# Hybrid encoder layer on one core: which buffers the first weight loads of the two down stages use, which queue writes the last sums of h, and in what order loads are asked for

## Chip, cores and metric

The kernel runs on one core of a Trainium2 chip. The metric is the device time of one execution in microseconds (us), the median of several runs. The core's engines are TensorE (PE in the profile, its weight loads PEld), VectorE (DVE), ScalarE (ACT), GpSimd (POOL) and SyncE (SP). A DMA is issued by an engine and stands in that engine's queue: "SPq" is what SP issues, "ACTq" what ScalarE issues. "L284" is line 284 of the kernel.

## The reference, cut to what matters

One encoder layer in float32 on 768 tokens (a prompt of 256 and a sample of 512), model width 1024. It has two feed-forward parts (FFN) around a mixer and a cross attention, each followed by a layer norm:

```python
def swiglu(x, w_gu, w_down):
    gate, up = jnp.split(x @ w_gu, 2, axis=-1)      # w_gu: 1024 x 5632
    return (jax.nn.silu(gate) * up) @ w_down        # w_down: 2816 x 1024

x = layer_norm(DN_ALPHA * x + 0.5 * swiglu(x, ffn1_w_gu[l], ffn1_w_down[l]), ...)
x = layer_norm(DN_ALPHA * x + parallel_mixer(x, ...), ...)
x = layer_norm(DN_ALPHA * x + memory_cross_attention(x, mem, ...), ...)
x = layer_norm(DN_ALPHA * x + 0.5 * swiglu(x, ffn2_w_gu[l], ffn2_w_down[l]), ...)
```

The change touches the second product of `swiglu`, `h @ w_down`, in both FFNs. There are thus two down stages, one near 340 us and one near 1630 us.

## The kernel before

**Precision.** Every float32 operand is split in a high and a low part (`split`: ScalarE copies the high part at L87, VectorE or GpSimd subtracts it at L88). A product is three matmuls: high by high, high by low, low by high. So a weight block `raw` becomes `wh` and `wl`, an activation becomes `hq` (both parts in one tile) or `ao`.

**The gate part** of an FFN makes the hidden units in 22 blocks j of 128 (all 768 tokens), with a scheme of seven products in place of eight on half matrices. TensorE writes into banks px, py, pz (L472), ScalarE snaps copies of them (`snap`, L477), VectorE adds them (`sum`, L484), ScalarE takes the SiLU (`sil`, L544), VectorE multiplies (`h`, L545). `gated` then splits h into `hq`, writes it to memory (`hspill`; not for the last four blocks, which stay on chip in `keep`), and for each pair of blocks makes four sums of its quarters (`hs`, L575 to L578), which go to memory as well (`sspill`). The sums of the very last block are not written where they are made: their stores are put in the list `late` and asked for inside `down_seven`, on SP's queue.

**The down part** is `down_seven` for 16 of the 22 blocks, in four groups d = 0 to 3, and `down_last` for the other six. In `down_seven` the products come in this order, each 18 matmuls of 128 x 512 at L284 into banks dn:

- 8 direct products: P1(0), P2(0), P1(1), P2(1), P1(2), P2(2), P2(3), P1(3). Group 0 takes its activations from `keep`, the others load them (768 KB, tile `ao`, a ring of four);
- sums V: four products on `y`, activations loaded as sums (384 KB, tile `sr`, three buffers) and split into `ao`; their weights are T, four kept blocks, plus a newly loaded one (L331);
- sums U, eight products (weights T again, L337, and a loaded block), sums Y, four (weights a sum of two loaded blocks);
- the last four direct products.

`add` (L294, L296) adds the banks into `acc`, the result, whose old values `load_acc` loads late, on ScalarE's queue (L1215).

Weight blocks of 512 KB are loaded by `loaded`. Of five in a row, two go into the buffers `raw7` of this function's own pool, three into the buffers with the tag "raw", which all weights of the kernel share; the pools' order decides what a load has to wait for, since the memory of `raw7` and of the T and ao tiles was used by the gate part before:

```python
            def loaded(q, d):
                turn[0] += 1
                if turn[0] % 5 < 2:
                    r = raw[turn[0] % 5]
                else:
                    r = wp.tile([128, 1024], F32, tag="raw", bufs=3, name=nid("raw"))
```

So the 1st, 5th, 6th, 10th, ... load takes a buffer of `raw7`. `ahead` loads the activations of `down_last` (`hr`, in the first stage four blocks, in the second six) before the last four direct products.

**What sets the order.** The kernel is written as a program, and a scheduler with buffers puts each engine's instructions in an order of its own; within one engine (and one queue) they then run in that order. `tc.issue_after(m)` makes the scheduler place instructions no earlier than m. `late_load` keeps its DMAs in program order. What stands behind a waiting DMA on a queue waits too.

Of the kernel before, what the change touches and what calls it, by code (L numbers as in the profile page):

```python
# [7 lines left out]
F32 = mybir.dt.float32  # L8
# [3 lines left out]
ALU = mybir.AluOpType  # L12
# [7 lines left out]
NFB = D_FF // 128  # L20
# [38 lines left out]
def _encoder(ctx, tc, nc, io, out, dbg):  # L59
# [158 lines left out]
            j = 2 * kp + kk  # L218
            tok_mm(ps, w, kk, hh[s.name, t, j], hl[s.name, t, j], first and kk == 0, stop and kk == 1, cols)

    def down_seven(n, wdn, pairs, keep, dr, sd, order6, load_acc, late, ahead):

        with tc.tile_pool(name=f"seven{n}", bufs=1, reuse_waits="tile") as pool:
            V = nc.vector
            nd = len(pairs)
            raw = [pool.tile([128, 1024], F32, name=nid("raw7")) for _ in range(2)]
            turn = [0]  # L230
            T = {d: pool.tile([128, 1024], F32, name=nid("T")) for d in range(nd)}
            bank = [psum(nid("dn")) for _ in range(8)]
            x, z, y = bank[0:3], bank[3:6], bank[6:8] + bank[3:4]

            def quadrant(dst, q, d):
                row, half = q
                kp = pairs[d][0]
                nc.sync.dma_start(dst.rearrange("p (a c) -> p a c", a=2),
                                  wdn[kp:kp + 2, half, :, row * 512:row * 512 + 512].rearrange("a p c -> p a c"))

            def loaded(q, d):
                turn[0] += 1
                if turn[0] % 5 < 2:
                    r = raw[turn[0] % 5]
                else:
                    r = wp.tile([128, 1024], F32, tag="raw", bufs=3, name=nid("raw"))
                quadrant(r[:], q, d)
                return r[:]
# [10 lines left out]
            def direct(t, par, d):  # L259

                if d == 0:
                    return [keep[2 * kp + par][:, t] for kp in pairs[d]]
                a = ring()
                kp = pairs[d][0]
                nc.sync.dma_start(a[:].bitcast(F32), dr[:, t, par, kp:kp + 2])
                return [a[:, k] for k in range(2)]

            def summed(s, d):
                r = pool.tile([128, 2, HT], F32, tag="sr", bufs=3, name=nid("sr"))
                kp = pairs[d][0]  # L270
                nc.sync.dma_start(r[:], sd[:, s, kp:kp + 2])
                a = ring()
                split(a[:, :, 0, :], a[:, :, 1, :], r[:])
                return [a[:, k] for k in range(2)]
# [25 lines left out]
            B11, B21, B12, B22 = (0, 0), (1, 0), (0, 1), (1, 1)  # L300
# [19 lines left out]
                P2(d)  # L320
            P2(own[-1])
            P1(own[-1])
            for spill in late:
                spill()
            for d in early:
                quadrant(T[d][:], B11, d)
            load_acc(1, 1)
            add(0, 0, z)
            add(0, 0, x)
            for d in sums_:  # L330
                V.tensor_tensor(T[d][:], T[d][:], loaded(B12, d), op=ALU.add)  # L331
                product(y, summed(0, d), weight(T[d][:]), d == sums_[0], d == sums_[-1])
            load_acc(0, 1)
            add(1, 1, y)
            for d in sums_:
# [5 lines left out]
                product(y, summed(2, d), weight(b22), False, d == sums_[-1])  # L341
            load_acc(1, 0)
            add(0, 1, y)
            for d in sums_:
                b12, b22 = loaded(B12, d), loaded(B22, d)
                V.tensor_tensor(b12, b12, b22, op=ALU.add)
                product(x, summed(3, d), weight(b12), False, d == sums_[-1])
            add(1, 1, x)
            ahead()
            for d in own:  # L350
                V.tensor_tensor(T[d][:], T[d][:], loaded(B21, d), op=ALU.add)
                product(x, direct(1, 1, d), weight(T[d][:]), False, d == own[-1])
# [158 lines left out]
    def ffn_fast(n, i, front, order6, src, groups, last):  # L511
# [35 lines left out]
            marks["dve"] = ins.ins  # L547
            gated(j, h32)

        h_of, late = {}, []  # L550

        def hq_tile(hs):
            if n == 1:
# [5 lines left out]
        def gated(j, h32):  # L559

            kp, par = j // 2, j % 2
            whole = par or kp in last
            hs = 2 if whole else 1
            h3 = h32[:].rearrange("p (t c) -> p t c", t=2)
            q = hq_tile(hs)
            split(q[:, :, 0, :], q[:, :, 1, :], h3[:, :hs, :])
            keep[j] = q
            h_of[j] = h3
            if j < NFB - 4:
                nc.sync.dma_start(dr[:, :hs, par, kp], q.bitcast(F32))  # L570
            if par and kp not in last:
                V = nc.vector
                (a11, a21), (a12, a22) = [[h_of[x][:, t, :] for t in range(2)] for x in (j - 1, j)]
                s_ = [glob["hs"].tile([128, HT], F32, tag="hs", bufs=3, name=nid("hs")) for _ in range(4)]
                V.tensor_tensor(s_[3][:], a11, a21, op=ALU.subtract)  # L575
                V.tensor_tensor(s_[0][:], a22, a21, op=ALU.subtract)
                V.scalar_tensor_tensor(s_[1][:], s_[0][:], -1.0, a11, ALU.mult, ALU.subtract)
                V.scalar_tensor_tensor(s_[2][:], s_[1][:], -1.0, a12, ALU.mult, ALU.subtract)  # L578

                def spill():  # L580
                    for x in (3, 0, 1, 2):
                        nc.sync.dma_start(sd[:, x, kp, :], s_[x][:])

                if j == NFB - 1:
                    late.append(spill)
                else:
                    spill()

        def plain_weights(j):
            rg, ru = [wp.tile([128, 1024], F32, tag="raw", bufs=3, name=nid("raw")) for _ in range(2)]  # L590
# [67 lines left out]
        else:  # L658
            lp = hlp.enter_context(tc.tile_pool(name="hlast", bufs=1, reuse_waits="tile"))
            ahead = lambda: load_h(js, lp, "hr", 6)  # L660
        down_seven(n, wdn, groups, keep, dr, sd, order6, load_acc, late, ahead)

        with tc.tile_pool(name=f"down{n}", bufs=1, reuse_waits="tile") as f2:
            if n == 1:
# [783 lines left out]
```

## Time and profile before

| | |
|---|---|
| median of 3 runs | 1814.77 us (1810.16 to 1815.77) |
| profiled execution | 1809.75 us, of which the span in the profile 1808.0 us |
| mean granted TensorE clock | 0.991 |
| TensorE busy | 1762.3 us, 97% of the span |
| weight loads of TensorE busy | 1618.6 us, 90% |
| VectorE busy | 1216.4 us, 67% |
| ScalarE busy | 763.8 us, 42% |
| DMA, mean | 148 GB/s |

The rows that the next parts show come from a timeline (start, us, engine, line, operation, output and inputs, and in brackets the engine's idle time ahead of the row and what ended it), from the list of waits (total us, number, longest), from the list of DMA issues (KB of one, median us from issue to landing) and from windows (length, then for each engine busy us and count, then granted clock, share of the 16 DMA engines, GB/s).

### The profile page before, as it was taken

Reading aid. Unit: us, or ns where it says so; the run is one execution under the profiler, and the core shown is the slowest. Engines: PE = TensorE matmul, PEld = TensorE weight load, DVE = VectorE, ACT = ScalarE, POOL = GpSimd, SP = SyncE. Lnnn points to the kernel's source line nnn. Section 1 sums busy time; section 2 is a strip of 40 time slices with the busy share of each in tenths; the row PEclk is TensorE's granted clock in tenths of the full one; section 3 lists DMA queues with packets and bytes.
Section 4 is the critical chain, followed back from the end, with each engine's and each line's share of the span. In section 5 each row is a group of like instructions: output and inputs, shape, how many; then the busy total and the mean of one; then the engine's idle time right before and its main releaser. Section 6 shows DMA issues by size and latency. Waiting matters only on the chain. (4 is left out here: it accounts for less than half of the span.)

```text
span 1808.0 us, 25217 instructions
## 1 busy us (share of the span) xinstructions
PE 1762.3 (97%) x9758; PEld 1618.6 (90%) x9758; DVE 1216.4 (67%) x2035; ACT 763.8 (42%) x1297; POOL 321.7 (18%) x186
## 2 busy tenths in 40 slices
PE   9999999899999999999999999999999999988998
PEld 9999999788889999888888888889899999986886
DVE  8777777377579553577664934585697777754856
ACT  6444454243135544645322244235344444432421
POOL 2000000000224002422244253244430000000012
PEclk9999999899999999999999999999999999998999
DMA  5434333597432333311463252255424343329951
GB/s 193 143 128 157 135 134 104 186 344 253 185 105 94 123 132 125 104 47 41 132 213 117 83 192 66 80 186 176 140 96 154 128 144 131 127 85 346 334 179 70
DMA packets 100535, 267.26 MB, mean 148 GB/s; under 512 B 10016, under 2 KB 23584, under 8 KB 100416
## 3 DMA queue, kind: packets, MB, share of 16 engines
q1 hardware_dynamic: 93504, 250.46, 39.9%
q10 hardware_dynamic: 6912, 15.21, 2.3%
q8 instruction: 76, 1.25, 0.3%
q14 instruction: 43, 0.35, 0.1%
HBM read 212.15 MB, written 53.48 MB: 147 GB/s over the span
## 5 line engine op out<-in xcount | busy, mean ns | idle before, releaser
L88 POOL TENSOR_TENSOR wl<-raw,wh 128x1024 fp32r<-128x1024 f32 (+1 forms) x94 | 231.6, 2468 | 1319.7 <-ACT wh L87 1271.4
L87 ACT ACTIVATE wh<-raw 128x512 fp32r<-128x512 f32 (+2 forms) x309 | 255.5, 830 | 330.0 <-PE to L108 81.6
L88 DVE TENSOR_TENSOR wl<-raw,wh 128x512 fp32r<-128x512 f32 (+2 forms) x215 | 182.8, 853 | 99.6 <-ACT wh L87 99.3
L284 PE MATMUL dn<-wh,ao 128*128 128x512 f32 x600 | 185.4, 389 | 0.0
L106 PE MATMUL pt<-xh,wh 128*128 128x512 f32 (+2 forms) x512 | 173.1, 338 | 0.0
L107 PE MATMUL pt<-xl,wh 128*128 128x512 f32 (+2 forms) x512 | 172.3, 337 | 0.0
L108 PE MATMUL pt<-xh,wl 128*128 128x512 f32 (+2 forms) x512 | 172.0, 336 | 0.0
L284 PEld LDWEIGHTS dn<-wh,ao 128*128 128x128 f32 x600 | 112.6, 188 | 23.5
L87 ACT ACTIVATE wh<-tt 128x512 fp32r<-128x512 f32 x156 | 95.3, 625 | 78.8 <-PE px L472 36.7
L284 PE MATMUL dn<-wl,ao 128*128 128x512 f32 x300 | 116.7, 389 | 0.0
L88 DVE TENSOR_TENSOR wl<-tt,wh 128x512 fp32r<-128x512 f32 x156 | 105.5, 689 | 2.2 <-ACT wh L87 0.5
L106 PEld LDWEIGHTS pt<-xh,wh 128*128 128x128 f32 x512 | 97.0, 189 | 9.7 <-issue 0.5
L108 PEld LDWEIGHTS pt<-xh,wl 128*128 128x128 f32 x512 | 97.0, 189 | 9.0
L107 PEld LDWEIGHTS pt<-xl,wh 128*128 128x128 f32 x512 | 97.1, 190 | 8.8 <-issue 0.2
L472 PE MATMUL px<-xh,wl 128*128 128x384 f32 x232 | 77.5, 334 | 0.0
L472 PE MATMUL px<-xh,wh 128*128 128x384 f32 x232 | 77.5, 334 | 0.0
L472 PE MATMUL px<-xl,wh 128*128 128x384 f32 x232 | 77.5, 334 | 0.0
L545 DVE SCALAR_TENSOR_TENSOR h<-sil,sum 128x384 f32<-128x384 f32 x78 | 43.5, 557 | 47.1 <-ACT sil L544 47.1
L544 ACT ACTIVATE sil<-sum 128x384 f32<-128x384 f32 x39 | 20.5, 526 | 125.9 <-DVE sum L484 125.9
L284 PEld LDWEIGHTS dn<-wl,ao 128*128 128x128 f32 x300 | 56.3, 188 | 11.8
L106 PE MATMUL dn<-wh,hr 128*128 128x512 f32 (+1 forms) x150 | 57.7, 385 | 0.0
L107 PE MATMUL dn<-wl,hr 128*128 128x512 f32 (+1 forms) x150 | 57.5, 383 | 0.0
(374 smaller groups left out, 4866.4 us busy)
## 6 DMA issues: line engine op xcount, KB each, us to landing
raw<-in_ffn_gu_dram SPq DMA_DIRECT2D x84, 512.0 KB, 3.5
raw<-in_ffn_dn_dram SPq DMA_DIRECT2D x64, 512.0 KB, 5.2
hspill<-hq SPq DMA_DIRECT2D x24, 768.0 KB, 3.7
raw<-in_w_mix_dram SPq DMA_DIRECT2D x32, 512.0 KB, 3.5
ao<-hspill SPq DMA_DIRECT2D x18, 768.0 KB, 5.7
sspill<-hs SPq DMA_DIRECT2D x64, 192.0 KB, 2.1
sr<-sspill SPq DMA_DIRECT2D x32, 384.0 KB, 5.7
hr<-hspill SPq DMA_DIRECT2D x24, 384.0 KB, 5.6
```

The costliest lines, as they stand in the source:

```text
L87: nc.scalar.activation(hi, src, AF.Copy)
L88: (lo_eng or nc.vector).tensor_tensor(lo, src, hi.bitcast(F32), op=ALU.subtract)
L106: nc.tensor.matmul(o, lh, rh, start=start, stop=False)
L107: nc.tensor.matmul(o, lh, rl, start=False, stop=False)
L108: nc.tensor.matmul(o, ll, rh, start=False, stop=stop)
L284: nc.tensor.matmul(ps[t][:], l, r[:, o], start=start and k == 0 and m == 0, stop=stop and k == 1 and m == 2, skip_group_check=True)
L472: nc.tensor.matmul(ps, l[:, c], r[:, k, :], start=st and n == 0, stop=sp_ and n == 2, skip_group_check=True)
L544: nc.scalar.activation(sil[:], g, AF.Silu)
L545: ins = nc.vector.scalar_tensor_tensor(h32[:, half * HT:(half + 1) * HT], sil[:], -0.5, u, ALU.mult, ALU.mult)
```

## The change

Four things, for both down stages:

1. `loaded` takes the buffers of `raw7` for the 4th, 5th, 9th, 10th, ... load, and the shared raw buffers for the others. So the first three weight blocks of a stage go to the shared buffers.
2. The four stores of the sums of the last block are issued where the sums are made, by ScalarE's queue in place of SP's. The list `late` is gone.
3. The loads of T for groups 0 and 1 and all of sums V (their weights and sums) may be placed only after the last load of the direct products (`issue_after(last_load)`). They were free before.
4. The loads of `ahead` (hr) may be placed only after the last load of sums of U.

```diff
             raw = [pool.tile([128, 1024], F32, name=nid("raw7")) for _ in range(2)]
-            turn = [0]
+            turn, last_load = [0], [None]
...
                 turn[0] += 1
-                if turn[0] % 5 < 2:
-                    r = raw[turn[0] % 5]
+                if turn[0] % 5 in (4, 0):
+                    r = raw[turn[0] % 5 // 4]
...
             def direct(t, par, d):
...
-                nc.sync.dma_start(a[:].bitcast(F32), dr[:, t, par, kp:kp + 2])
+                last_load[0] = nc.sync.dma_start(a[:].bitcast(F32), dr[:, t, par, kp:kp + 2])
...
             def summed(s, d):
...
-                nc.sync.dma_start(r[:], sd[:, s, kp:kp + 2])
+                last_load[0] = nc.sync.dma_start(r[:], sd[:, s, kp:kp + 2])
...
             P1(own[-1])
-            for spill in late:
-                spill()
-            for d in early:
-                quadrant(T[d][:], B11, d)
             load_acc(1, 1)
             add(0, 0, z)
             add(0, 0, x)
-            for d in sums_:
-                V.tensor_tensor(T[d][:], T[d][:], loaded(B12, d), op=ALU.add)
-                product(y, summed(0, d), weight(T[d][:]), d == sums_[0], d == sums_[-1])
+            with tc.issue_after(last_load[0].ins):
+                for d in early:
+                    quadrant(T[d][:], B11, d)
+                for d in sums_:
+                    V.tensor_tensor(T[d][:], T[d][:], loaded(B12, d), op=ALU.add)
+                    product(y, summed(0, d), weight(T[d][:]), d == sums_[0], d == sums_[-1])
...
             add(0, 1, y)
+            hold = last_load[0].ins
             for d in sums_:
                 b12, b22 = loaded(B12, d), loaded(B22, d)
...
-            ahead()
+            with tc.issue_after(hold):
+                ahead()
...
-                def spill():
-                    for x in (3, 0, 1, 2):
-                        nc.sync.dma_start(sd[:, x, kp, :], s_[x][:])
-                if j == NFB - 1:
-                    late.append(spill)
-                else:
-                    spill()
+                queue = nc.scalar if j == NFB - 1 else nc.sync
+                for x in (3, 0, 1, 2):
+                    queue.dma_start(sd[:, x, kp, :], s_[x][:])
```

How it moves the instructions. On ScalarE, at the end of the second stage's gate part (snap, sil and hq are the last gate block's, wh the splits of down weights), before:

```order
L477 ACTIVATE snap_15213<-px_15200 128x384
L477 ACTIVATE snap_15228<-py_15215 128x384
L477 ACTIVATE snap_15242<-px_15200 128x384
L544 ACTIVATE sil_15300<-sum_15285 128x384
L544 ACTIVATE sil_15303<-px_15200 128x384
L87 ACTIVATE hq_15306<-h_15299 128x2x384
L87 ACTIVATE wh_15346<-raw_15332 128x1024
L1215 DMA acc<-x_8740 128x512 x3
L87 ACTIVATE wh_15373<-raw_15371 128x1024
L87 ACTIVATE wh_15399<-raw_15395 128x1024
```

and now:

```order
L87 ACTIVATE wh_15352<-raw_15350 128x1024
L582 DMA sspill_12017<-hs_15313 128x384
L478 ACTIVATE snap_15214<-px_15201 128x384
L87 ACTIVATE wh_15379<-raw_15377 128x1024
L478 ACTIVATE snap_15229<-py_15216 128x384
L478 ACTIVATE snap_15243<-px_15201 128x384
L87 ACTIVATE wh_15405<-raw_15401 128x1024
L545 ACTIVATE sil_15301<-sum_15286 128x384
L545 ACTIVATE sil_15304<-px_15201 128x384
L1210 DMA acc<-x_8741 128x512
L87 ACTIVATE hq_15307<-h_15300 128x2x384
L582 DMA sspill_12017<-hs_15310 128x384
```

The splits of the first three down weights moved from behind the last hq to between the snaps and the SiLUs of that block, and the stores of the sums joined this queue.

On SP's queue, at the start of the second down stage, before (raw_15332 is the first weight block of the stage in the order of use, raw_15395 and raw_15423 the third and fourth, ao the activations of the direct products):

```order
L238 DMA raw_15395<-in_ffn_dn_dram 128x2x512
L238 DMA raw_15423<-in_ffn_dn_dram 128x2x512
L582 DMA sspill_12016<-hs_15312 128x384
L653 DMA hr_16050<-hspill_12015 128x768 x2
L582 DMA sspill_12016<-hs_15309 128x384
L582 DMA sspill_12016<-hs_15310 128x384
L582 DMA sspill_12016<-hs_15311 128x384
L653 DMA hr_16053<-hspill_12015 128x768 x2
L238 DMA raw_15332<-in_ffn_dn_dram 128x2x512
L265 DMA ao_15397<-hspill_12015 128x1536
```

and now, where raw_15377 and raw_15401 are the second and third weight block, raw_15337 the fourth, and raw_15504 one of the last of the direct products:

```order
L237 DMA raw_15377<-in_ffn_dn_dram 128x2x512
L237 DMA raw_15401<-in_ffn_dn_dram 128x2x512
L237 DMA raw_15504<-in_ffn_dn_dram 128x2x512
L264 DMA ao_15403<-hspill_12016 128x1536
L264 DMA ao_15427<-hspill_12016 128x1536
L237 DMA raw_15337<-in_ffn_dn_dram 128x2x512
L237 DMA T_15340<-in_ffn_dn_dram 128x2x512
L264 DMA ao_15453<-hspill_12016 128x1536
```

The stores and the four hr loads are gone from this place; no load of the first weights stands behind them any more, and the fourth weights stand behind two ao loads. In the first stage the same place reads now:

```order
L237 DMA raw_3527<-in_ffn_dn_dram 128x2x512
L237 DMA raw_3630<-in_ffn_dn_dram 128x2x512
L264 DMA ao_3529<-hspill_83 128x1536
L264 DMA ao_3553<-hspill_83 128x1536
L237 DMA raw_3463<-in_ffn_dn_dram 128x2x512
L237 DMA T_3466<-in_ffn_dn_dram 128x2x512
L264 DMA ao_3579<-hspill_83 128x1536
L264 DMA ao_3603<-hspill_83 128x1536
```

Here too raw_3463, the fourth weights, stands two ao loads behind the first.

On VectorE, at the end of the direct products of the second stage (T and wl for the first product of sums V are T_15334 and wl_15571), before:

```order
L88 TENSOR_TENSOR wl_15526<-T_15336,wh_15525 128x1024
L331 TENSOR_TENSOR T_15334<-T_15334,raw_15562 128x1024
L88 TENSOR_TENSOR ao_15567<-sr_15565,ao_15567 128x2x384
L331 TENSOR_TENSOR T_15335<-T_15335,raw_15592 128x1024
L296 SCALAR_TENSOR_TENSOR acc<-acc,dn_15340 128x512
L88 TENSOR_TENSOR wl_15571<-T_15334,wh_15570 128x1024
L296 SCALAR_TENSOR_TENSOR acc<-acc,dn_15341 128x512
```

and now (T_15339 and wl_15573):

```order
L88 TENSOR_TENSOR wl_15532<-T_15341,wh_15531 128x1024
L295 SCALAR_TENSOR_TENSOR acc<-acc,dn_15345 128x512
L295 SCALAR_TENSOR_TENSOR acc<-acc,dn_15346 128x512
L295 SCALAR_TENSOR_TENSOR acc<-acc,dn_15347 128x512
L330 TENSOR_TENSOR T_15339<-T_15339,raw_15564 128x1024
L293 TENSOR_TENSOR acc<-acc,dn_15342 128x512
L293 TENSOR_TENSOR acc<-acc,dn_15343 128x512
L88 TENSOR_TENSOR ao_15569<-sr_15567,ao_15569 128x2x384
L293 TENSOR_TENSOR acc<-acc,dn_15344 128x512
L88 TENSOR_TENSOR wl_15573<-T_15339,wh_15572 128x1024
```

All six additions into acc (L295 and L293) stand ahead of the split wl_15573 now, of which one stood ahead before.

On SP's queue in the second stage, ahead of the last four products, now (raw_16070, and those behind it, are their weights):

```order
L270 DMA sr_16022<-sspill_12017 128x768
L648 DMA hr_16055<-hspill_12016 128x768
L648 DMA hr_16058<-hspill_12016 128x768 x2
L648 DMA hr_16061<-hspill_12016 128x768 x2
L648 DMA hr_16064<-hspill_12016 128x768 x2
L648 DMA hr_16067<-hspill_12016 128x768 x2
L237 DMA raw_16070<-in_ffn_dn_dram 128x2x512
```

Before, single hr loads stood between the loads of weights and sums of the products ahead.

More of the change, by code (lines that the diff above doesn't have):

```diff
@@ L219, in down, with down_seven @@
             tok_mm(ps, w, kk, hh[s.name, t, j], hl[s.name, t, j], first and kk == 0, stop and kk == 1, cols)
-    def down_seven(n, wdn, pairs, keep, dr, sd, order6, load_acc, late, ahead):
+    def down_seven(n, wdn, pairs, keep, dr, sd, order6, load_acc, ahead):
         with tc.tile_pool(name=f"seven{n}", bufs=1, reuse_waits="tile") as pool:
@@ L548, in block @@
             gated(j, h32)
-        h_of, late = {}, []
+        h_of = {}
         def hq_tile(hs):
@@ L660, in ffn_fast @@
             ahead = lambda: load_h(js, lp, "hr", 6)
-        down_seven(n, wdn, groups, keep, dr, sd, order6, load_acc, late, ahead)
+        down_seven(n, wdn, groups, keep, dr, sd, order6, load_acc, ahead)
         with tc.tile_pool(name=f"down{n}", bufs=1, reuse_waits="tile") as f2:
```

## The prediction

> **What bounds the kernel now.** I read the times first, then the page's busy shares, the waits of TensorE, the timeline at the two places that they point to, and the windows around them. The first two lines are the page's; the others are waits of TensorE (us in total, times, the longest):
>
> ```profile
> span 1808.0 us, 25217 instructions
> PE 1762.3 (97%) x9758; PEld 1618.6 (90%) x9758; DVE 1216.4 (67%) x2035; ACT 763.8 (42%) x1297; POOL 321.7 (18%) x186
> ...
> PE dn L284 <- ACT wh L87: 20.8, 2, 11.9
> PE px L472 <- ACT snap L477: 4.3, 2, 3.5
> ```
>
> TensorE is busy for 97% of the span, and more than half of the idle time that anything releases is two waits of dn, the product of the down stages. Both are at the first matmul of a down stage. The timeline of the second start (start, us, engine, line, tile, and in brackets the idle time before and its releaser):
>
> ```profile
> 1602.28 0.38 SPq L238 DMA_DIRECT2D raw<-in_ffn_dn_dram  x1
> ...
> 1621.06 0.34 PE L472 MATMUL px<-xh,wl 128*128 128x384 f32 x1
> 1621.28 0.81 SPq L653 DMA_DIRECT2D hr<-hspill  x2
> ...
> 1623.19 2.25 SPq L582 DMA_DIRECT2D sspill<-hs  x3
> ...
> 1623.68 0.95 DVE L88 TENSOR_TENSOR hq<-h,hq 128x768 fp32r<-128x768 f32 x1
> 1624.54 0.55 DVE L578 SCALAR_TENSOR_TENSOR hs<-hs,h 128x384 f32<-128x384 f32 x1
> 1625.48 0.94 SPq L653 DMA_DIRECT2D hr<-hspill  x2
> 1626.76 0.38 SPq L238 DMA_DIRECT2D raw<-in_ffn_dn_dram  x1
> 1627.26 0.88 SPq L265 DMA_DIRECT2D ao<-hspill  x2
> ...
> 1632.20 1.06 ACT L87 ACTIVATE wh<-raw 128x1024 fp32r<-128x1024 f32 x1 [8.76 <-DMA raw<-in_ffn_dn_dram]
> 1632.21 1.50 ACTq L1215 DMA_DIRECT2D acc<-x  x3
> 1633.31 1.22 PE L284 MATMUL dn<-wh,hq 128*128 128x512 f32 x2 [11.92 <-ACT wh L87]
> ```
>
> TensorE ends the last gate product at 1621.4. The load of the first down weights is issued only at 1626.76, behind three stores of sums and two pairs of hr loads on SP's queue, while weights of later products were fetched from 1602.28 on and lie unused. It lands at 1632.2, is split in 1.06 us, and TensorE goes on 11.92 us late. The first down stage is the same with fewer loads ahead:
>
> ```profile
> 323.63 16.65 SPq L582 DMA_DIRECT2D sspill<-hs  x4
> 335.90 0.34 PE L472 MATMUL px<-A22h,wl 128*128 128x384 f32 x1
> 339.39 0.55 DVE L578 SCALAR_TENSOR_TENSOR hs<-hs,h 128x384 f32<-128x384 f32 x1
> 340.39 0.38 SPq L238 DMA_DIRECT2D raw<-in_ffn_dn_dram  x1
> 345.11 1.22 PE L284 MATMUL dn<-wh,hq 128*128 128x512 f32 x2 [8.87 <-ACT wh L87]
> 356.58 0.39 PE L284 MATMUL dn<-wh,ao 128*128 128x512 f32 x1
> 1640.17 0.40 PE L284 MATMUL dn<-wl,hq 128*128 128x512 f32 x1
> 1644.15 0.40 PE L284 MATMUL dn<-wh,ao 128*128 128x512 f32 x1
> ```
>
> The rows at 356.58 and 1644.15 are the first matmul of the third product, 36 matmuls behind the start; 1640.17 stands 17 matmuls ahead of the latter. What the granted clock did there, from the windows (length, busy time and count of PE, PEld, DVE, ACT, POOL, then PEclk, DMA share, GB/s):
>
> ```profile
> 345.10:350.10 5.00, 4.95 (x11) 3.46 (x12) 4.71 (x4) 2.95 (x3) 0.00 (x0) 0.50 1.02 397
> 1633.30:1638.30 5.00, 4.95 (x12) 3.47 (x13) 4.67 (x4) 2.95 (x3) 0.00 (x0) 0.54 1.02 409
> 1638.30:1643.30 5.00, 5.00 (x23) 4.04 (x22) 1.27 (x2) 1.06 (x1) 0.00 (x0) 1.00 1.03 405
> 1669.20:1685.60 16.40, 16.40 (x74) 13.59 (x73) 16.40 (x18) 8.34 (x10) 0.00 (x0) 1.00 0.92 323
> ```
>
> After the wait the clock is at half for about five us. The DMA engines are full (1.02) at about 400 GB/s, so a 512 KB weight block costs them 1.3 us, a 768 KB ao block 2.0 and a 384 KB one 1.0.
>
> **The two waits (first loads into the common buffers, stores off SP's queue).** The first three weight blocks now sit in the common raw buffers, are fetched in the last gate block and split in it. The splits, three of 1.06 us on ScalarE and of 1.2 on VectorE, lie in idle time of that block:
>
> ```profile
> 1615.26 0.56 DVE L484 TENSOR_TENSOR sum<-snap,py 128x384 f32<-128x384 f32 x1 [6.49 <-PE py L472]
> 1620.00 0.53 ACT L544 ACTIVATE sil<-sum 128x384 f32<-128x384 f32 x1 [6.40 <-DVE sum L484]
> ```
>
> 6.4 us of each engine stand free there, so I cost them at nothing; without that cover the gate sums would come 1 to 2 us late. The first product needs only kept tiles of earlier blocks and can start at 1621.4; the second needs hq, done at 1624.63, before the 18 matmuls of the first end at 1621.4 + 4.2 = 1625.6. Both waits go: 8.87 + 11.92 = 20.8 us.
>
> The half clock goes with them. 36 matmuls took 356.58 - 345.11 = 11.47 us and 1644.15 - 1633.31 = 10.84. At full clock, 23 matmuls in the 5 us window and some records missing, I take (1644.15 - 1640.17) / 17 = 0.234 us each, so 8.43 us (a product of 18 is 4.2); the slow start cost 3.0 and 2.4, together 5.4. The Trainium skill (TensorE: Matmul & The Clock Gate, Part 1) says that the clock falls to half after an idle window of about 3.4 us and returns after about 3.4 us of work; by it the loss would be an estimated 1.7 us a stage, 3.4 in all, and the sum 2 us smaller. The trace agrees on the rule and shows the longer value.
>
> Gross: 20.8 + 5.4 = 26.2 us.
>
> The four stores and three acc loads go through ScalarE's queue: by the 1.50 us row of three, 0.5 us each, 2.0 us more of ScalarE, between the last hq and the first split that is still to do. ScalarE idled 8.76 us there. What is queued behind the last store (it waits for the row at 1624.54, done at 1625.1) is two acc loads and the split of the fourth weights, which land later. Nothing.
>
> **What is late next: the direct products.** Now ao and the fourth weights must keep pace with a TensorE that starts 9 to 12 us earlier, while their buffers come free at the same time as before. The order shows for the first stage that the first ao load waits for the last sum (339.39 + 0.55 = 339.94) and the fourth weights stand two places behind it.
>
> ```profile
> 340.89 0.89 SPq L265 DMA_DIRECT2D ao<-hspill  x2
> raw<-in_ffn_gu_dram SPq DMA_DIRECT2D x84, 512.0 KB, 3.5
> ao<-hspill SPq DMA_DIRECT2D x18, 768.0 KB, 5.7
> ```
>
> A 512 KB load on free engines lands in 3.5 us, 2.2 more than its transfer. The first ao is issued at 340.0 and lands at 340.0 + 2.2 + 2.0 plus about 0.8 of acc loads and stores that share the engines: 345.0, against a need at 336.2 + 2 x 4.2 = 344.7. The second lands at 347, the fourth weights at 348.4; split, their high part is ready at 349.5 and the low part at 350.7. TensorE wants them at 345.0 + 4.2 = 349.2, has three matmuls (0.7 us) that need the high part alone, and so loses 0.3 there and 0.5 at the low part. With the first ao 1.1; I take 1.5. Bounds: 0, if the stores land early, and 4.7, if all 4 us of the four stores and three acc loads (768 KB each set) go ahead, not 0.8. The next ones have 2 us of room or more, at 1.3 or 2.0 us of transfer against 4.2 us of product.
>
> In the second stage the first ao waits only for a matmul of the last block some 6 us before its end, and four hr loads, 4 us of transfer, no longer stand ahead. The second ao at 1625.2 lands at 1630, the fourth weights at 1631.5, split at 1633.8, against 1634.0. I take 0, bounds 0 and, with those 3.2 us ahead, 3.2.
>
> **What is late next: the first product of sums.**
>
> ```profile
> 1661.21 1.23 DVE L331 TENSOR_TENSOR T<-T,raw 128x1024 f32<-128x1024 f32 x1 [10.45 <-DMA raw<-in_ffn_dn_dram]
> 1663.06 0.96 DVE L88 TENSOR_TENSOR ao<-sr,ao 128x768 fp32r<-128x768 f32 x1 [0.62 <-ACT ao L87]
> 1665.07 0.68 DVE L296 SCALAR_TENSOR_TENSOR acc<-acc,dn 128x512 f32<-128x512 f32 x1
> 1665.67 1.22 DVE L88 TENSOR_TENSOR wl<-T,wh 128x1024 fp32r<-128x1024 f32 x1
> ...
> 1671.80 1.22 DVE L331 TENSOR_TENSOR T<-T,raw 128x1024 f32<-128x1024 f32 x1
> 1672.93 0.95 DVE L88 TENSOR_TENSOR ao<-sr,ao 128x768 fp32r<-128x768 f32 x1
> 1673.80 1.22 DVE L331 TENSOR_TENSOR T<-T,raw 128x1024 f32<-128x1024 f32 x1
> ```
>
> Before, VectorE adds T at 1661.2 and splits it at 1665.7, some 3 us before the direct products end near 1669.4 (1644.15 and six more of 4.2). Now, by the order, it first does all six additions into acc, the last of which needs the last direct matmul. From that end: addition 0.6, split 1.2, so wl stands 2.0 us after it (with 0.1 of handing over). TensorE has three matmuls, 0.7 us, to do without it, and waits 1.3. The second product of sums has T, ao, T and wl ahead, 1.1 + 0.9 + 1.1 + 1.2, ends 6.3 us after and is wanted at 1.3 + 4.2 + 0.7 = 6.2; later ones gain room, since a product takes VectorE 3.1 us (1.13 + 0.87 + 1.13, from start to start) against TensorE's 4.2. So 1.35 us a stage, 2.7 in all; bounds 0, as before, and 3.2 a stage, if the addition of T and the split of ao come late too. A gain is excluded, since TensorE waits nowhere in this phase now.
>
> **The hr loads of the second stage** (held until the last sums are asked for): nine of them, 8.8 us of transfer, now stand in one row on SP's queue ahead of the last four weight blocks. They are asked for some 14 us before TensorE reaches the last group of sums, and the weights behind them are wanted 16 us after that. I cost it at nothing; with that room gone up to 9 us.
>
> **The sum.** 26.2 - 1.5 - 0 - 2.7 = 22.0 us. The profiled execution took 1809.75 us, 1.75 beside its span of 1808.0; it gives 1787.7. It is 5 us below the median of the three runs, 1814.77, of which one is at 1810.16; on the median it gives 1792.8. I take 1790. The bounds of the first three terms give gains of 12 to 26 us, with the hr row 3.
>
> **Rivals.**
> (1) The transfers become the bound in the direct products. For it: the engines are full at 1.02 in these windows, and the ao and weights now come into a shorter time. Against: 1.3 to 2.0 us of transfer for each half of a 4.2 us product, and 4 us of hr loads gone. Then 4.7 and 3.2 us of waits, with 2 us of half clock behind them, 8 more than in my sum: a gain of 14, 1796 to 1801. The Trainium skill (DMA: Bandwidth & Descriptors, Where 436 GB/s comes from) puts the limit of such loads at 358 GB/s; the rows show 397 to 409, so the measurement decides against it here.
> (2) The hr row is in the way of the last weights: 5 to 9 us back in the second stage, 1795 to 1799. For it, their place ahead in the queue; against it, 16 us and more of room.
> (3) The start is not freed: another wait (a buffer of wh, or hq) holds the first product as long. Against: the order puts the splits ahead, and hq is done at 1624.63. Time as before.
> (4) Slower: VectorE becomes the bound through the sums. It is busy for 16.40 of 16.40 us there with a lead of 8 us, and the change takes the lead away. If a product took it over 4.2 us in place of 3.1 to 3.3, that is its point of decision, each of 12 products of the two phases in both stages would wait; with 1.3 us for each, 31 us, 5 more than the gross gain: 1815 to 1820.
>
> **How the numbers follow.** Forecast 0.70, rival (1) 0.15, (2) 0.06, (3) 0.05, (4) 0.04. A measurement of this kernel tells about 0.3%, 5.4 us, from no change. Forecast, (1) and (2) lie beyond it: faster 0.91; (3) is the same, 0.05; (4) slower, 0.04. The range takes 1782, the gross gain without any loss on the profiled time with 1.5 us of spread, to 1801, the far end of (1) and of (2); the forecast's own is 1783 to 1796.
>
> **What would show it.** No wait of dn for wh at the two starts, granted clock 1.00 there, the first dn matmul within 0.3 us of the last px; a wait of dn for wl of 1 to 1.5 us at the first product of sums in each stage; about 1 us at the fourth product of the first stage, none in the second. Wrong if dn waits for ao by more than 3 us, for wl in product after product, or if the last four products wait for raw.

## The result, and the profile after

The changed kernel takes 1793.14 us (median of 4 runs, 1790.46 to 1795.52) against 1813.39 (4 runs, 1810.16 to 1815.77): 0.9889 of the time, with an interval of 0.9866 to 0.9912. In two later comparisons it took 1794.13 and 1792.16 us, 0.9903 (0.9879 to 0.9927) and 0.9893 (0.9878 to 0.9909). The forecast was 1790, in a range of 1782 to 1801. The change is faster, by about 20 us.

The page of the changed kernel (span, busy shares) and its waits of TensorE in dn (us in total, times, the longest):

```profile
span 1793.7 us, 25220 instructions
PE 1762.4 (98%) x9758; PEld 1618.4 (90%) x9758; DVE 1216.5 (68%) x2035; ACT 763.9 (43%) x1297; POOL 322.3 (18%) x186
...
PE dn L283 <- DVE wl L88: 3.0, 3, 1.3
...
PE dn L283 <- DMA ao<-hspill: 1.6, 1, 1.6
...
PE dn L283 <- ACT wh L87: 0.4, 1, 0.4
```

The two waits of 20.8 us for the first weights are gone; 5.0 us of smaller ones have come. The timeline at the two starts, and the first waits behind the first one:

```profile
336.22 0.34 PE L473 MATMUL px<-A22h,wl 128*128 128x384 f32 x1
336.40 0.39 PE L283 MATMUL dn<-wh,hq 128*128 128x512 f32 x1
...
340.32 0.81 SPq L264 DMA_DIRECT2D ao<-hspill  x2
...
346.55 0.50 PE L283 MATMUL dn<-wh,ao 128*128 128x512 f32 x1 [1.56 <-DMA ao<-hspill]
351.32 0.98 PE L283 MATMUL dn<-wh,ao 128*128 128x512 f32 x3 [0.36 <-ACT wh L87]
352.58 0.50 PE L283 MATMUL dn<-wl,ao 128*128 128x512 f32 x1 [0.28 <-DVE wl L88]
...
1619.11 0.34 PE L473 MATMUL px<-xh,wl 128*128 128x384 f32 x1
1619.28 0.39 PE L283 MATMUL dn<-wh,hq 128*128 128x512 f32 x1
```

The first dn matmul stands 0.18 us behind the last px, where it stood 9.21 and 12.25 us behind. The windows of the same two places (columns as in the prediction) show the full clock:

```profile
336.40:341.40 5.00, 5.00 (x23) 4.03 (x23) 3.01 (x5) 1.34 (x2) 0.00 (x0) 1.00 0.55 174
341.40:346.40 5.00, 3.59 (x16) 2.56 (x14) 0.00 (x0) 0.00 (x0) 0.00 (x0) 1.00 0.98 353
1619.20:1624.20 5.00, 5.00 (x23) 4.04 (x22) 3.01 (x5) 1.34 (x2) 0.00 (x0) 1.00 0.53 163
```

TensorE's matmuls stand in the same order in both kernels but for a few, so a stage can be measured from start to start: from the last px matmul to the first matmul behind the 28 products, dn<-wh,hr. Those ends, before and after:

```profile
462.80 0.39 PE L106 MATMUL dn<-wh,hr 128*128 128x512 f32 x1
1750.44 0.39 PE L106 MATMUL dn<-wh,hr 128*128 128x512 f32 x1
```
```profile
456.01 0.39 PE L106 MATMUL dn<-wh,hr 128*128 128x512 f32 x1
1736.21 0.39 PE L106 MATMUL dn<-wh,hr 128*128 128x512 f32 x1
```

So the first stage took 462.80 - 335.90 = 126.90 us and takes 119.79; the second took 129.38 and takes 117.10. Together 256.28 and 236.89: 19.4 us. This measure tells the variants apart more finely than the whole time does. From the starts of every 18th matmul, in us (product 9 is the first of the sums V; a product without any wait is 4.08, the first three 4.22, 4.21 and 4.10):

| kernel | whole time, median | stages, sum | stage 1: start, products 1 to 4, 9 | stage 2: the same |
|---|---|---|---|---|
| before | 1813.39 | 256.28 | 9.21; 7.25 4.22 4.08 4.08; 4.08 | 12.25; 6.62 4.22 4.09 4.08; 4.08 |
| changed | 1793.14 | 236.89 | 0.18; 4.22 5.93 4.77 4.80; 5.72 | 0.18; 4.22 4.21 4.10 4.51; 5.72 |
| changed, again | 1794.13 | 236.78 | 0.18; 4.22 5.89 5.12 4.79; 5.76 | 0.18; 4.22 4.21 4.10 4.08; 5.76 |
| changed, third | 1792.16 | 236.37 | 0.18; 4.22 5.09 4.76 4.80; 5.72 | 0.18; 4.22 4.21 4.14 4.80; 5.76 |
| part 1 alone | 1801.80 | 243.11 | 0.18; 4.22 8.73 5.54 4.08; 4.08 | 0.18; 4.22 8.39 6.93 4.11; 4.38 |
| part 2 alone | 1808.72 | 251.44 | 5.56; 6.20 4.22 4.09 4.08; 4.08 | 12.38; 6.44 4.21 4.08 4.08; 4.08 |
| without part 2 | 1798.05 | 241.97 | 0.18; 4.22 6.58 5.81 4.08; 5.74 | 0.18; 4.22 7.17 5.69 4.08; 5.74 |
| without part 3 | 1792.25 | 236.22 | 0.18; 4.22 6.24 4.83 4.79; 4.40 | 0.18; 4.22 4.21 4.19 4.79; 4.40 |
| without part 4 | 1803.41 | 248.56 | 0.18; 4.22 8.37 6.78 4.08; 5.76 | 0.18; 4.22 10.63 6.02 4.08; 5.74 |
| split ahead of additions | 1793.21 | 236.39 | 0.18; 4.22 6.13 5.84 4.09; 5.04 | 0.18; 4.22 4.21 4.10 4.64; 4.71 |
| acc loads later | 1796.26 | 238.33 | 0.18; 4.22 4.39 4.30 4.80; 7.45 | 0.17; 4.22 4.21 4.10 4.08; 5.32 |
| other memory for ao | 1789.10 | 233.38 | 0.18; 4.22 4.21 4.10 4.08; 5.76 | 0.18; 4.22 4.21 4.10 4.08; 5.67 |
| the same, without part 3 | 1788.33 | 230.99 | 0.18; 4.22 4.21 4.10 4.08; 4.36 | 0.18; 4.22 4.21 4.10 4.08; 4.36 |

### The profile page after: what moved, and what is told of

Read it like the earlier page. It is cut to its first block, busy times and chain, and to the rows that moved or that the text cites. A ratio compares the mean times of both kernels' runs of the same rounds, so it can differ in the third digit from the quotient of the medians.

```text
span 1793.7 us, 25220 instructions
## 1 busy us (share of the span) xinstructions
PE 1762.4 (98%) x9758; PEld 1618.4 (90%) x9758; DVE 1216.5 (68%) x2035; ACT 763.9 (43%) x1297; POOL 322.3 (18%) x186
```

## Experiments: the change part by part

The theory is that part 1 frees the starts, and that parts 2 and 4 keep the loads of ao, which the freed TensorE then waits for next, from standing behind other work. Rivals: the stores on SP's queue were what held the weights, or one part does it all.

**Part 1 alone.**

```diff
-                if turn[0] % 5 < 2:
-                    r = raw[turn[0] % 5]
+                if turn[0] % 5 in (4, 0):
+                    r = raw[turn[0] % 5 // 4]
```

> The kernel before with the first part of the change alone (first three weight loads into the common raw buffers; stores stay on SP's queue; no order of loads). Theory: the splits come early and the two starts are freed (no wait of dn for wh at the first product, 20.8 us gone, half clock there gone), but in the order SP's queue now holds two more weight loads, three hr loads (384 KB each, the first waits until the first product has read the hq tiles it overwrites, 340.4 us) and the stores ahead of the first ao load. So TensorE runs two products and then waits for ao: about 5 us and a half-clock stretch of 2 to 3 us in each stage are given back. 1801 to 1806 us, 7 to 12 us faster than before. Rival (the gain is the buffers' alone, edits 2 to 4 are worth nothing): 1793, as the whole change. Rival (the stores are what held the first weights): little or no gain, above 1808.

Measured: 1801.80 us (1798.72 to 1805.72), 0.9944 of before (0.9925 to 0.9962). Both starts are freed (0.18 us), and two waits of the third product for ao take their place. SP's queue and TensorE in the first stage of this kernel, and TensorE's wait in the second:

```profile
340.36 0.32 SPq L653 DMA_DIRECT2D hr<-hspill  x1
341.08 0.32 SPq L582 DMA_DIRECT2D sspill<-hs  x1
341.47 0.93 SPq L653 DMA_DIRECT2D hr<-hspill  x2
343.24 0.81 SPq L265 DMA_DIRECT2D ao<-hspill  x2
...
349.61 0.80 PE L284 MATMUL dn<-wh,ao 128*128 128x512 f32 x1 [4.36 <-DMA ao<-hspill]
1630.02 0.80 PE L284 MATMUL dn<-wh,ao 128*128 128x512 f32 x1 [4.02 <-DMA ao<-hspill]
```

The ao loads stand behind the stores, which wait for sums, and behind hr loads, which wait for the first product to have read the hq tiles that they overwrite. Behind each wait a matmul runs 0.80 us long in place of 0.50: the half clock is back. Part 1 gains 13.2 of the 19.4 us of the stages.

**Part 2 alone.**

```diff
-                if j == NFB - 1:
-                    late.append(spill)
-                else:
-                    spill()
+                queue = nc.scalar if j == NFB - 1 else nc.sync
+                for x in (3, 0, 1, 2):
+                    queue.dma_start(sd[:, x, kp, :], s_[x][:])
```

> The kernel before with the second part alone (last stores on ScalarE's queue). Theory: in the first stage the load of the first weights, still into raw7, has nothing late ahead of it on SP's queue any more (its memory is free about 20 us before), so the wait of 8.9 us goes, and the half clock with it; about 10 us. In the second stage five hr loads stand ahead of it, which cannot start before the gate part's last products end (1621), and the weights take a completion slot after the first of them: they land near 1630 instead of 1632, the wait is 9 to 10 us in place of 11.9. Together 10 to 13 us faster, 1800 to 1803. Rival (the stores are off the path): no change, 1813. Rival (the stores hold the weights in both stages): 20 us, 1793.

Measured: 1808.72 us (10 runs), 0.9981 (0.9972 to 0.9990). It is faster, by 3.8 us where I expected 10 to 13. In the first stage the weights land early, as expected (issued at 330.28), but the wait only falls from 9.2 to 5.6 us. ScalarE of this kernel, and TensorE:

```profile
338.26 2.27 ACTq L582 DMA_DIRECT2D sspill<-hs  x3
340.58 1.06 ACT L87 ACTIVATE wh<-raw 128x1024 fp32r<-128x1024 f32 x1 [2.06 <-DMA sspill<-hs]
...
341.69 1.22 PE L284 MATMUL dn<-wh,hq 128*128 128x512 f32 x2 [5.23 <-ACT wh L87]
```

The stores now stand on ScalarE's queue ahead of the split of the first weights and wait there for the last sum. I had counted the queue that they leave and not the one that they join. In the second stage, five hr loads are in flight when the weights are issued:

```profile
1619.21 2.24 SPq L648 DMA_DIRECT2D hr<-hspill  x5
1622.68 0.38 SPq L238 DMA_DIRECT2D raw<-in_ffn_dn_dram  x1
...
1631.36 1.22 PE L284 MATMUL dn<-wh,hq 128*128 128x512 f32 x2 [12.04 <-ACT wh L87]
```

Issued 3.5 us behind the first of them, they are split only at 1630.3, and nothing is gained there. The first rival holds in half of one stage only.

**Without part 4** (hr loads free).

```diff
-            with tc.issue_after(hold):
-                ahead()
+            ahead()
```

> The changed kernel without its fourth part (hr loads free again). Theory: in the order three hr loads in the first stage and six in the second stand ahead of the first or second ao load again; TensorE waits for ao 5 to 6 us in the first stage in place of 1.6, and 3 to 5 us in the second in place of none, with half clock behind the longer wait: 8 to 12 us slower than the changed kernel, 1801 to 1805. Rival (hr loads hide, the DMA engines have room): 1793, no difference.

Measured: 1803.41 us, 0.9953 (0.9938 to 0.9968), 11.7 us more in the stages than the changed kernel. The two waits:

```profile
347.66 0.80 PE L283 MATMUL dn<-wh,ao 128*128 128x512 f32 x1 [3.99 <-DMA ao<-hspill]
1632.71 0.80 PE L283 MATMUL dn<-wh,ao 128*128 128x512 f32 x1 [6.25 <-DMA ao<-hspill]
```

The loss as a whole came as expected, the two waits did not: 5 to 6 us were expected in the first stage and 3 to 5 in the second. So the hold, a part without any gain of its own in my sum, is worth 11.7 us beside the others.

**Without part 2** (stores on SP's queue, the rest as changed).

```diff
-                queue = nc.scalar if j == NFB - 1 else nc.sync
+                queue = nc.sync
```

> The changed kernel with the last stores of sums back on SP's queue (no second part). Theory: the first weights no longer need that part, since they are loaded before the stores; what the stores hold now is the ao loads behind them. First stage: the first ao waits for the last sum anyway, so 0.3 to 1 us more. Second stage: the first ao, issued at 1613 in the changed kernel, waits for the last sum too and comes 2 to 3 us late. Wait of dn for ao 4 to 5 us in all in place of 1.6; 2 to 4 us slower than the changed kernel, 1796 to 1798. Rival (that part is worth nothing beside the others): 1793 to 1794. Rival (stores are what held the weights): the wait of dn for wh at the start comes back, above 1800.

Measured: 1798.05 us, 0.9920 (0.9904 to 0.9937), 5.1 us more in the stages: just above what was expected: the waits (5.0 us) came out as expected, and the half clock behind them had not been counted. SP's queue in the second stage, TensorE's two waits, and windows of one us behind the first of them (the two left out are at 0.50 like the second row):

```profile
1618.54 2.25 SPq L582 DMA_DIRECT2D sspill<-hs  x3
1620.90 1.15 SPq L264 DMA_DIRECT2D ao<-hspill  x2
...
346.98 0.50 PE L283 MATMUL dn<-wh,ao 128*128 128x512 f32 x1 [2.21 <-DMA ao<-hspill]
1627.96 0.80 PE L283 MATMUL dn<-wh,ao 128*128 128x512 f32 x1 [2.79 <-DMA ao<-hspill]
```
```profile
347.00:348.00 1.00, 1.00 (x4) 0.85 (x5) 0.00 (x0) 0.00 (x0) 0.00 (x0) 0.87 1.06 412
348.00:349.00 1.00, 1.00 (x3) 0.78 (x3) 0.00 (x0) 0.00 (x0) 0.00 (x0) 0.50 1.08 420
...
351.00:352.00 1.00, 1.00 (x5) 0.79 (x5) 0.69 (x1) 0.70 (x2) 0.00 (x0) 0.92 1.02 418
```

**Without part 3's order of T and the sums V.**

```diff
-            with tc.issue_after(last_load[0].ins):
+            if True:
```

> The changed kernel without the first half of the order of loads (T and the loads of the sums V free again, hr loads still held). Theory: only two weight loads come ahead of the ao loads, and their buffers are free before the gate part ends, so the direct products do not change (within 0.5 us); the addition of T moves up on VectorE, and the wait of 1.34 us at the first product of sums shrinks to 0 to 0.8 in each stage: 1791 to 1794, 0 to 2.5 us faster than the changed kernel. Rival (this part guards the ao loads as the hold of hr does): 4 to 10 us slower, waits of dn for ao.

Measured: 1792.25 us, 0.9889 (0.9869 to 0.9909), the same as the changed kernel by the whole time. Product 9 takes 4.40 us in place of 5.72 in both stages, as expected; the direct products took about as long (20.1 against 19.7 us for the first four in the first stage, 17.4 against 17.0 in the second). This order does not guard the ao loads. The stages together are only 0.7 us shorter, though (236.22). In the second one TensorE waits 0.71 us for an addition into acc among the last four products, which it does not in the changed kernel, and products 24 and 25 take 9.9 us there in place of 8.3.

## Experiments: the two losses that are left

**VectorE at the first product of sums.** The program's order is turned round, so that the low split of T stands ahead of the last three additions:

```diff
             add(0, 0, z)
-            add(0, 0, x)
...
+                    s0, w0 = summed(0, d), weight(T[d][:])
+                    if d == sums_[0]:
+                        with tc.issue_after(last_split[0].ins):
+                            add(0, 0, x)
+                    product(y, s0, w0, d == sums_[0], d == sums_[-1])
```

> The changed kernel with VectorE's order turned round at the start of the sums: T's addition, the split of ao and the low split of T for the first product of sums stand ahead of the three last additions into acc (direct products' x), the program's order apart from that kept. Theory (the wait there is VectorE's order): the first product of sums takes 4.1 to 4.6 us in place of 5.7 in each stage, 2.2 to 3.2 us in all: 1790 to 1792. Rival (T's weights or the sums land too late anyway): the wait stays, 1793 to 1794. Rival (the later additions hold the bank of the next products): another wait takes its place, the same time.

Measured: 1793.21 us, 0.9888 (0.9871 to 0.9904). Product 9 takes 5.04 and 4.71 us in place of 5.72 twice, 1.7 us less, with waits of 0.62 and 0.30 left. The whole time does not tell it from no change, and the stages together are only 0.5 us shorter. The third product of the first stage took 1.1 us longer in this profile, at half clock behind the wait for ao (the last section shows it). In the second stage TensorE waits 0.63 us for an addition into acc at the first of the last four products, and products 24 to 26 take 0.9 us more: the second rival came in part, at another place. The mechanism holds, its size is smaller than expected. In the changed kernel itself, VectorE and the wait read:

```profile
369.17 1.22 DVE L330 TENSOR_TENSOR T<-T,raw 128x1024 f32<-128x1024 f32 x1
...
371.89 0.95 DVE L88 TENSOR_TENSOR ao<-sr,ao 128x768 fp32r<-128x768 f32 x1
372.76 0.68 DVE L293 TENSOR_TENSOR acc<-acc,dn 128x512 f32<-128x512 f32 x1
373.36 1.22 DVE L88 TENSOR_TENSOR wl<-T,wh 128x1024 fp32r<-128x1024 f32 x1
...
374.63 0.50 PE L283 MATMUL dn<-wl,ao 128*128 128x512 f32 x1 [1.34 <-DVE wl L88]
```

**The late ao of the first stage: is it the acc loads that share the DMA engines?**

```diff
-                if d == 0:
+                if d == 2:
                     load_acc(0, 0)
```

> The changed kernel with the first three loads of old acc values (768 KB) asked for after the sixth direct product's loads in place of the first's. Theory (the late ao in the first stage shares the DMA engines with acc loads and stores): 2.0 us of transfer leave the place, the second, third and fourth products of the first stage take 13.0 to 14.3 us in place of 15.5 (12.4 without any wait): 1.2 to 2.5 us faster in the first stage, nothing in the second; 1790.5 to 1792.5. Rival (the ao waits for its own issue after the last sum, the engines have room): 15.5 us as before.

Measured: 1796.26 us, 0.9908 (0.9894 to 0.9923), not faster than the changed kernel. Products 2 to 4 take 13.49 us in place of 15.50, as expected. But the first stage as a whole takes 121.12 us in place of 119.79, since the first sums and their weights come late (this kernel, first stage):

```profile
349.93 1.43 ACTq L1210 DMA_DIRECT2D acc<-in_x_tok_dram  x3
360.78 1.52 ACTq L1210 DMA_DIRECT2D acc<-in_x_tok_dram  x3
...
372.30 0.96 PE L283 MATMUL dn<-wh,ao 128*128 128x512 f32 x3 [1.57 <-ACT wh L87]
374.60 0.50 PE L283 MATMUL dn<-wl,ao 128*128 128x512 f32 x1 [1.34 <-DVE wl L88]
```

The gain is given back behind the place where it was made. SP waits 5.6 us here for one of the moved loads to land before it issues a load of T (at 360.82; the changed kernel issues it at 357.17), and the first weights and sums behind that are issued at 361.26 and 361.77 in place of 358.55 and 359.82. Behind the two waits shown the clock falls to half: it is 0.71 in 375 to 376, 0.50 in the next two us and 0.58 in 378 to 379, which is 3.42 us at half and costs half of that, 1.7 us.

**Or is it the memory of ao, which the last sum holds until 340 us?**

```diff
+            first_ao = [pool.tile([128, 2, 2, HT], F32R, tag="ao", bufs=4, name=nid("ao"))]
             raw = [pool.tile([128, 1024], F32, name=nid("raw7")) for _ in range(2)]
...
             def ring():
+                if first_ao:
+                    return first_ao.pop()
```

> The changed kernel with the first ao tile taken from the pool ahead of raw7 and T, nothing else: its memory is then that which the gate part's S4 tiles leave near 330 us, and the fourth weights' raw7 takes the memory that waits for the last sum (340 us). Theory (the first stage loses 3.1 to 3.5 us since the first ao load, issued at 340.3, and the weights behind it come 10 us later than their turn): both first ao loads are issued before 333 us in the first stage, products 2 to 4 take 12.4 to 12.8 us in place of 15.5; 2.7 to 3.3 us off the first stage, nothing off the second, whose waits of dn for wl stay: 1789 to 1792. Rival (the transfers bound the direct products, as in the runs before the loads would pile up elsewhere): the third to sixth product wait in turn, 15 us and more as before, 1793 to 1795.

Measured: 1789.10 us, 0.9878 (0.9861 to 0.9894). SP's queue of this kernel and its waits in dn:

```profile
328.63 0.81 SPq L267 DMA_DIRECT2D ao<-hspill  x2
338.57 0.38 SPq L238 DMA_DIRECT2D raw<-in_ffn_dn_dram  x1
...
PE dn L286 <- DVE wl L88: 2.5, 2, 1.3
```

No wait for ao or wh is left. The first stage takes 116.71 us, 3.1 less, and products 2 to 4 take 12.39; the second stays at 116.67. So the late issue was the cause: with an early one the transfers do not bound the direct products. What made it costly is shown by the run before, where 2.0 of these 3.1 us went when the acc loads were out of the way.

**Both together.**

> The same, and T and the loads of sums V free again (no first half of the order of loads). Theory: the gains add up, since the one is in the direct products and the other at the first product of sums: stage one 115.3 to 116.5 us, stage two 115.5 to 116.5 (from the last gate matmul to the end of the 28 products; 114.4 is 28 products at 4.08 without any wait), 24 to 26 us below the kernel before, 1786 to 1790. Rival (more loads ahead of ao eat it up, as with the hr loads): 1791 to 1795.

Measured: 1788.33 us (1786.88 to 1790.07), 0.9870 (0.9855 to 0.9885). The stages take 115.12 and 115.87 us, 25.3 below before; the gains add up (233.38 - 230.99 = 2.4), but for 0.75 us that product 25 of the second stage takes longer. This beats both kernels by the stages, by 5.9 us against the changed one beside 3.8 in the medians of that comparison (1792.16).

**The changed kernel again, twice.**

> The changed kernel once more, for its spread and a second profile: 1790 to 1796 us. Its first profile showed a half-clock stretch in the mixer near 827 us and other losses outside of the down stages, some 5 us together, that the kernel before did not show in its one profile. Theory: these are the run's, not the change's, and are missing or elsewhere in this profile; rival: they come back at the same place, as a consequence of the earlier start of the mixer.

> The changed kernel a third time, beside the two variants: 1791 to 1795 us, stages of 119.5 to 120.3 and 116.5 to 117.3 us. The half-clock stretch near 827 us, seen in both of its profiles and not in that of the kernel before: if it is the run's, it is missing here or elsewhere; if it follows from the change, it is there again.

The sum of its stages repeats within 0.5 us, and the whole time within 2 us. Each stage by itself repeats less well: those of the third run, 118.93 and 117.44 us, both lie just outside of what was expected. The stretch near 827 us is told of below.

## Why the prediction was right, and where its sizes were off

- **The two waits, 20.8 us:** right. From start to start 9.21 + 12.25 - 2 x 0.18 = 21.1 us went, and the splits in the last gate block cost it nothing: TensorE's waits of px for snap were 4.3 us in total before and are 4.1 now.
- **The half clock, 5.4 us:** right. Products 1 and 2 took 7.25 + 4.22 and 6.62 + 4.22; without a wait they take 8.43, the figure of the prediction, as the second stage shows (4.22 + 4.21). That is 3.04 and 2.41.
- **Seven DMAs on ScalarE's queue, nothing:** right for this kernel, where the splits stand ahead of them. Part 2 alone shows the price when they don't.
- **Direct products, 1.5 us in the first stage:** the place was right and the size too small. Products 2 to 4 take 15.50 us against 12.39: 3.1 us (3.4 and 2.3 in the two other profiles). The issue at 340.3 was forecast to 0.3 us; the transfer was not. The first ao, forecast at 345.0, is what TensorE waited for until 346.55. The term for loads in flight together was too small: 0.8 us for stores and acc loads. The sum reckons 5.0 us from the issue of the first ao to its landing, where the row of ao loads that it shows has a median of 5.7, and 6.2 us went by until TensorE could start. With the acc loads moved away products 2 to 4 take 13.49 us. The bound of 4.7 held it.
- **Direct products, 0 in the second stage:** 0.4, 0 and 0.75 us in the three profiles of the changed kernel.
- **First product of sums, 1.35 us a stage:** the wait is 1.34 us in both. Products 9 and 10 together take 1.8 us more than 8.16 (5.72 + 4.27), so the whole term was 3.7 us and not 2.7: the second product of sums, forecast to be just in time, takes 0.2 us more than 4.08, and product 9 takes 0.3 us more than its wait explains (5.72 - 4.08 - 1.34). I had not put that in, and no run shows its cause.
- **The hr row, nothing:** right. No wait of TensorE stands between 1690 and 1750 us.
- **The sum:** 22.0 us forecast in the stages, 19.4 measured. By the profiled executions the whole gain was 14.2 us (1809.75 to 1795.52), by the medians 20.3: the profiled execution of before lay 3.6 us below its median, that of after 2.4 above. The other 5 us of the profiled pair lie outside of both stages, 4.8 of them between (from the end of the first to the last px: 1621.06 - 462.80 = 1158.26 us before, 1619.11 - 456.01 = 1163.10 after); the largest piece is told of below. The forecast from the median, 1792.8, lies 0.3 us from the measured median, and that is luck in part: the sum was 2.6 us too large in the stages, and the median of before from which it was taken was 1.4 us above the one of the four runs here.
- **The rivals:** (1), transfers as the bound, was half there, at a third of its price, and the other memory for ao shows that it was a late issue. (2) to (4) did not come: VectorE kept its pace behind the first two products of sums. What the prediction did not see is that the hr loads would have cost 11.7 us had they not been held; it priced only what the hold could cost.

## What to carry to other kernels

When a wait is removed, write down what each engine asks for next, and look at what stands ahead of that in its queue: here the gain of the freed weights was 13 us with the other loads left in the way, 19 with them held, and 23 with the next buffer in memory that came free early. A DMA that is moved to another queue delays what stands behind it there, so look at both queues. Of two buffers with different earlier owners, give the one that comes free first to the transfer that is needed first.

## What the runs showed of the hardware that I had not expected

A wait of 1.8 us can be enough for the half clock. In the kernel without part 2, whose windows of one us stand above, the clock is 0.87 in 347 to 348, 0.50 in the three windows up to 351, and 0.92 in 351 to 352. A mean of 0.87 is 0.26 us at half and 0.92 is 0.16, so it was at half from 347.74 to 351.16, for 3.42 us. The wait before it lasted 2.21 us and ended at 346.98. Behind the wait of 2.79 us in the second stage the same sum gives 3.42 us again. Behind the waits of 1.34 and 1.56 us of the changed kernel it stayed at 1.00. Two more waits lie between. The first row and the windows are of the kernel with the split ahead of the additions, the last row is of the one without part 3:

```profile
346.03 0.50 PE L283 MATMUL dn<-wh,ao 128*128 128x512 f32 x1 [1.76 <-DMA ao<-hspill]
347.00:348.00 1.00, 1.00 (x4) 0.77 (x4) 0.00 (x0) 0.00 (x0) 0.00 (x0) 0.57 0.99 375
...
350.00:351.00 1.00, 1.00 (x5) 0.82 (x4) 0.15 (x1) 0.81 (x1) 0.00 (x0) 0.73 1.03 428
```
```profile
348.08 0.50 PE L283 MATMUL dn<-wh,ao 128*128 128x512 f32 x1 [1.87 <-DMA ao<-hspill]
```

Behind the wait of 1.76 us the clock was at half for 3.4 us, from 347.14 to 350.54. Behind the longer one of 1.87 us it stayed at 1.00.

The Trainium skill (TensorE: Matmul & The Clock Gate, Part 1) has the clock follow the activity in windows of 3413 ns that run freely, and has it fall after an idle one. The length agrees with the 3.42 us. That such a window must be idle throughout does not: the 3.42 us ahead of 347.74 held 2.21 us of waiting and 1.2 us of work, and those ahead of 347.14 held 1.76 us of waiting. The measurement decides: in these stages a wait is to be budgeted from about 1.7 us on, not from 3.4, and two shorter ones close together, 1.57 and 1.34 us in the kernel with the acc loads later, brought the half clock too. That the 1.87 us did no harm would fit windows that run freely, if this wait lay in two of them; no run shows by itself where they lie.

The mixer has a place near 827 us where TensorE pauses several times. There the clock was full in 5 of the 13 profiles and fell for a while in 8, which lengthens that place by 1.4 to 2.9 us (2.9 in the profile of the changed kernel above, of its 4.8). Windows of before (which does this work 7 us later), of the changed kernel, and of the kernel with other memory for ao:

```profile
833.00:839.00 6.00, 5.88 (x53) 5.54 (x54) 5.68 (x16) 5.55 (x11) 0.00 (x0) 1.00 0.01 3
```
```profile
826.00:832.00 6.00, 5.67 (x34) 5.35 (x35) 4.86 (x13) 4.41 (x10) 0.00 (x0) 0.52 0.00 0
```
```profile
823.00:828.00 5.00, 5.00 (x45) 4.66 (x43) 4.68 (x14) 4.56 (x10) 0.00 (x0) 1.00 0.01 3
```

All three profiles of the changed kernel have it (0.52, 0.72 and 0.72 in 826 to 832), and that of before has not. The kernel with other memory for ao, whose mixer starts earlier still, has not either, and part 2 alone has it. So an earlier start does not bring it by itself; whether the change makes it likelier stays open. Near 1030 us the clock falls in 3 of the 13 profiles and near 1200 us in 7, which costs 1.5 us each time. The profile of before is one of only two in which it falls nowhere between the two down stages, so some of its short span there is luck.
